# Moving some stick-breaking products from the vector engine to GpSimd in a Hymba encoder block

## The chip, the cores and the metric

The kernel runs on one core of a Trainium2 chip. A core has a matrix engine (PE, with its weight loads shown apart as PEld), a vector engine (DVE), a scalar engine for activations (ACT), GpSimd (POOL) and a queue engine (SP) that here issues nearly all DMAs. Each engine carries out its own instructions strictly in the order in which they stand in its program; semaphores hold an instruction until what it needs is done. The metric is the device time of one execution in microseconds (us), smaller is better. The kernel before takes 2757.65 us (median of 3 runs, 2754.74 to 2759.51).

## The reference

One layer of an encoder block over 2048 tokens of width 1024, batch 1: an RMS norm, one projection into six parts, differential attention (4 heads), stick-breaking attention (8 heads of width 64), an output projection added to the input, then a second norm and a gated feed-forward of width 2816, added again. The part that the change touches is stick-breaking attention, for query t and key s before it:

```python
z = jnp.einsum('bqhd,bkhd->bhqk', qb, k).astype(jnp.float32) * scale
mask = (k_pos[None, :] < q_pos[:, None])[None, None]
log_1mb = jnp.where(mask, jax.nn.log_sigmoid(-z), 0.0)
rem = lax.cumsum(log_1mb, axis=3, reverse=True) - log_1mb
a = jnp.where(mask, jnp.exp(jax.nn.log_sigmoid(z) + rem), 0.0)
return jnp.einsum('bhqk,bkhd->bqhd', a.astype(v.dtype), v)
```

In words: the weight of key s is sigmoid(z) at s, times the product of sigmoid(-z) over all keys between s and t.

## The kernel before

Work runs in groups g = 0 to 7. Groups 0 to 3 are one differential head each, groups 4 to 7 two stick-breaking heads each. While the attention of group g runs, the projection of group g + 1 is interleaved with it; beside g = 7, which has no projection after it, stands the output projection (`out_proj`, L766 its matmuls) with the second norm and the operands of the feed-forward (`post`, `x_ops`). The feed-forward follows, bound by PE throughout. Nearly every f32 operand is kept as a pair of f16 values, hi and lo, and each product of pairs is three matmuls.

One step of stick-breaking attention (`stage_a`) takes a block of 128 queries, one of two heads and up to 1024 keys: a tile. There are 48 tiles and 80 chunks of up to 512 keys in a group. A chunk goes through:

- PE computes the scores into a PSUM bank `sc` (L453; on the diagonal one more matmul, L455). There are four such banks.
- ACT writes sigmoid(-z) to the SBUF tile `om` (L559) and then sigmoid(z) over the scores in PSUM (L560).
- DVE runs the product from the last key back to the first in place in `om` (L562, a scan; its second operand `sc` is read and not used).
- DVE multiplies sigmoid(z) from PSUM with the scan shifted by one key, into the SBUF tile `be` (L563).

When the tile's chunks are done (`split_t`), ACT or POOL casts `be` to f16 (L89 on ACT), POOL subtracts to get the lo half (L98), and SP issues a DMA transpose of the pair into `aT` (L408). PE multiplies `aT` with the values (L463, `stage_b`), five tiles later in the written order. The SBUF tiles `be` and `om` come from one ring of nine (`z4`), the f16 pairs from a ring of three (`s16`), `aT` from a ring of five.

Two things set the order. The program is written as generators that interleave the attention with the projection; a scheduler then simulates it and fixes the order on each engine. And which engine gets a piece of work is often picked at build time by a planner: a load in ns for ACT (A), DVE (D) and POOL (P), set to zero at every fourth query block (`level`), added to by `note` for work with a fixed place and by `pick` for the rest, which takes the engine with the least load after it:

```python
def pick(**cost):
    e = min(cost, key=lambda k: load[k] + cost[k] * KW[k])
    load[e] += cost[e] * KW[e]
    return e
```

The planner also places the projection's PSUM evictions. `split_psum` picks ACT (L332) or DVE (L334) for the f16 hi half, and DVE always does the lo half (L335). `tt`, whose instructions all stand at L98, picks DVE or POOL for the sums of `x_ops`.

Of the kernel before, what the change touches and what calls it, by code (L numbers as in the profile page):

```python
# [15 lines left out]
AF = mybir.ActivationFunctionType  # L16
ALU = mybir.AluOpType
# [4 lines left out]
S, D, P = 2048, 1024, 128  # L22
# [37 lines left out]
def block(tc, a, out):  # L60
    nc = tc.nc
    PE, ACT, DVE, POOL, SP = nc.tensor, nc.scalar, nc.vector, nc.gpsimd, nc.sync
    top = ExitStack()
    with top:
# [8 lines left out]
        def note(e, ns):  # L73
            load[e] += ns * KW[e]
# [6 lines that stand above are left out]
        def level():  # L81
            for k in load:
                load[k] = 0.0
# [16 lines left out]
        def pri(k):  # L100
            def deco(f):
                @functools.wraps(f)
                def g(*args):
                    with tc.high_priority(PRI[k]) if PRI[k] else nullcontext():
                        return f(*args)
                return g
            return deco

        def nm(s):
            uid[0] += 1  # L110
            return f"{s}{uid[0]}"
# [144 lines left out]
        with ExitStack() as ph1:  # L256
# [6 lines left out]
            def z4():  # L263
                return zp.tile([P, 1028], F32, tag="z4", bufs=ZB, name=nm("z4"))
# [137 lines left out]
            @pri("spl")  # L402
            def split_t(src, n, he="ADP", le="DP"):
                s16 = s16p.tile([P, 2048], F16, tag="s16", bufs=SB, name=nm("s16"))
                to16(s16[:, :n], src, n, he)
                tt(s16[:, n : 2 * n], src, s16[:, :n], ALU.subtract, n, le)
                aT = sp.tile([P, 16, P], F16, tag="aT", bufs=AB, name=nm("aT"))
                SP.dma_start_transpose(aT[:, : 2 * n // P, :], s16[:, : 2 * n])  # L408
                return aT
# [36 lines left out]
            def fq(g, i):  # L446
                k = 2 if g == NG - 1 else 4
                return (i % k, k)

            @pri("sc")  # L450
            def score_chunk(G, sc, i, q, m, w, cut=False):
                for o in range(2):
                    PE.matmul(sc[:, : 128 * w].rearrange("p (t n) -> p t n", n=P), lhsT=G["q"][i // 4][:, 2 - 2 * o + m, i % 4, :], rhs=G["k"][q][:, m, 0:w, :], start=o == 0, stop=o == 1)  # L453
                if cut:
                    PE.matmul(sc[:, 128 * w - P : 128 * w], lhsT=idb[:], rhs=tri[:], start=False, stop=True, skip_group_check=True)  # L455

            @pri("pv")
            def pv(G, yp, y0, aT, b, n, o, wd, start, stop):
                nb = n // P
                for j in range(nb):  # L460
                    v = G["v"][2 * b + j // 4][:, j % 4, :]
                    for q, (a_, v_) in enumerate(((j, o), (j, o + wd), (nb + j, o))):
                        PE.matmul(yp[:, y0 : y0 + wd], lhsT=aT[:, a_, :], rhs=v[:, v_ : v_ + wd], start=start and j == 0 and q == 0, stop=stop and j == nb - 1 and q == 2, skip_group_check=True)  # L463
# [77 lines left out]
            def sb_attn(g, G):  # L541
                last = {}

                @pri("at")
                def stage_a(i, m, b):
                    L = (i + 1) * 128
                    n = min(1024, L - 1024 * b)
                    be, om = z4(), z4()
                    if b == i // 8:
                        DVE.memset(om[:, n : n + 1], 8192.0)  # L550
                    else:
                        DVE.tensor_copy(om[:, n : n + 1], last[m][:, 0:1])
                    last[m] = om
                    for c in range((n - 1) // 512, -1, -1):
                        lo, hi = 512 * c, min(512 * c + 512, n)
                        w = hi - lo
                        sc = ps.tile([P, 512], F32, tag="sc", bufs=4, name=nm("sc"))
                        score_chunk(G, sc, i, 2 * b + c, m, w // P, b == i // 8 and hi == n)
                        ACT.activation(om[:, lo:hi], sc[:, :w], AF.Sigmoid, scale=G["nkz"][:])  # L559
                        ACT.activation(sc[:, :w], sc[:, :w], AF.Sigmoid, scale=G["kz"][:])  # L560
                        ov = om[:, lo:hi][:, ::-1]
                        DVE.tensor_tensor_scan(ov, ov, sc[:, :w], om[:, hi : hi + 1], op0=ALU.mult, op1=ALU.bypass)  # L562
                        DVE.tensor_tensor(be[:, lo:hi], sc[:, :w], om[:, lo + 1 : hi + 1], ALU.mult)  # L563
                        note("A", 1.7 * w + 400)
                        note("D", 3.15 * w + 350)
                    return n, split_t(be[:, :n], n, "A", "P")

                ypd = {}

                def stage_b(i, m, b, n, aT):  # L570
                    r, k = fq(g, i)
                    if i // k not in ypd:
                        ypd[i // k] = ps.tile([P, 512], F32, tag="yp", name=nm("yp"))
                    yp = ypd[i // k]
                    pv(G, yp, P * r + 64 * m, aT, b, n, 128 * m, 64, r == 0 and m == 0 and b == i // 8, r == k - 1 and m == 1 and b == 0)
                    if m == 1 and b == 0 and r == k - 1:
                        finish(g, G, i, k, yp)
                        G["fin"] = i + 1

                pend = []  # L580
                done = 0
                for i in range(NT):
                    if i % 4 == 0:
                        level()
                    for b in range(i // 8, -1, -1):
                        for m in range(2):
                            n, aT = stage_a(i, m, b)
                            pend.append((i, m, b, n, aT))
                            if len(pend) > PD:
                                stage_b(*pend.pop(0))  # L590
                            done += n // P + CS
                            yield done / (272 + 48 * CS), (i + 1 if b == 0 and m == 1 else i)
                for u in pend:
                    stage_b(*u)
# [640 lines left out]
```

## Time and profile before

| what | value |
|---|---|
| median of the timed runs | 2757.65 us |
| the profiled execution's own time | 2755.86 us |
| its span, first to last instruction | 2754.1 us |
| busy over the span: PE, DVE, POOL, ACT | 90%, 73%, 53%, 49% |
| mean granted PE clock | 0.966 |
| first to last scan (L562), that is groups 4 to 7 | 612.6 to 1395.6 us |

A row of groups reads: line, engine, operation, output and input tiles, shape and count, then busy us and the mean ns of one, then the us that the engine stood idle just before them and what ended it. A row of waits reads: who waited, for whom, us in total, times, longest. A row of stretches gives, for a stretch of time, its length, the busy us of PE, PEld, DVE, ACT and POOL with the number of instructions in brackets, the granted clock, the share of the DMA engines that packets took (several may overlap, so it can exceed 1), and GB/s.

### The profile page before, as it was taken

Reading aid. Unit: us, or ns where it says so; the run is one execution under the profiler, and the core shown is the slowest. Engines: PE = TensorE matmul, PEld = TensorE weight load, DVE = VectorE, ACT = ScalarE, POOL = GpSimd, SP = SyncE. Lnnn points to the kernel's source line nnn. Section 1 sums busy time; section 2 is a strip of 40 time slices with the busy share of each in tenths; the row PEclk is TensorE's granted clock in tenths of the full one; section 3 lists DMA queues with packets and bytes.
Section 4 is the critical chain, followed back from the end, with each engine's and each line's share of the span. In section 5 each row is a group of like instructions: output and inputs, shape, how many; then the busy total and the mean of one; then the engine's idle time right before and its main releaser. Section 6 shows DMA issues by size and latency. Waiting matters only on the chain. (4 is left out here: it accounts for less than half of the span.)

```text
span 2754.1 us, 45485 instructions
## 1 busy us (share of the span) xinstructions
PE 2491.4 (90%) x17084; PEld 1411.9 (51%) x17084; DVE 1997.4 (73%) x3782; ACT 1361.3 (49%) x2543; POOL 1447.6 (53%) x1008
## 2 busy tenths in 40 slices
PE   7998989888888786888989899999999999999998
PEld 4665555555555453457775444444444444444443
DVE  6898879787889989986655877777785544444445
ACT  4665656566878778765644535444352212111121
POOL 2578767655455545546565656565574232322323
PEclk9999999999999987999999999999999999999999
DMA  6788787789999988987797675656658834635534
GB/s 225 201 170 184 148 189 163 173 172 203 196 217 191 198 175 156 199 196 208 199 272 273 218 241 199 220 196 226 235 182 307 315 146 164 229 136 198 207 121 167
DMA packets 649133, 551.91 MB, mean 200 GB/s; under 512 B 506624, under 2 KB 574208, under 8 KB 638672
## 3 DMA queue, kind: packets, MB, share of 16 engines
q1 hardware_dynamic: 647088, 546.92, 72.0%
q8 instruction: 134, 2.20, 0.3%
q0 software_dynamic: 512, 1.36, 0.2%
q10 hardware_dynamic: 1312, 0.72, 0.1%
q14 instruction: 87, 0.71, 0.1%
HBM read 265.27 MB, written 151.52 MB: 151 GB/s over the span
## 5 line engine op out<-in xcount | busy, mean ns | idle before, releaser
L98 POOL TENSOR_TENSOR s<-z,s 128x1024 f16<-128x1024 f32 (+7 forms) x288 | 473.9, 1653 | 334.1 <-ACT s L89 291.2
L325 PE MATMUL pj<-w,xt 128*128 128x384 f16 x3072 | 572.2, 334 | 29.3 <-DVE st L335 12.1
L325 PEld LDWEIGHTS <-xt 128*128 128x128 f16 x3072 | 300.2, 100 | 239.9 <-issue 37.3
L453 PE MATMUL sc<-kT,qT 128*128 128x512 f16 (+3 forms) x1280 | 348.7, 363 | 72.0 <-DVE z L563 33.0
L1041 PE MATMUL pd<-wd,act 128*128 128x512 f16 x1848 | 406.0, 379 | 3.4 <-DVE hs L1047 2.4
L562 DVE TENSOR_TENSOR_SCAN z<-z,sc 128x512 f32<-128x512 f32 (+3 forms) x320 | 355.5, 1113 | 69.4 <-ACT sc L560 67.5
L463 PE MATMUL yp<-v,aT 128*128 128x64 f16 (+1 forms) x4896 | 282.0, 208 | 76.4 <-DMA aT<-s 75.7
L463 PEld LDWEIGHTS <-aT 128*128 128x128 f16 x4896 | 246.5, 102 | 165.1 <-DMA aT<-s 101.7
L943 PEld LDWEIGHTS <-wg 128*128 128x128 f16 x1848 | 182.3, 99 | 247.3 <-issue 37.3
L1041 PEld LDWEIGHTS <-act 128*128 128x128 f16 x1848 | 180.7, 98 | 222.3 <-issue 4.6
L943 PEld LDWEIGHTS <-wu 128*128 128x128 f16 x1848 | 181.8, 98 | 219.7 <-issue 7.2
L98 POOL TENSOR_TENSOR hs<-hs,cu 128x512 f32<-128x512 f32 x132 | 166.8, 1268 | 239.8 <-DVE cu L1047 86.3
L98 POOL TENSOR_TENSOR act<-cg,act 128x512 f16<-128x512 f32 x117 | 166.6, 1437 | 231.4 <-ACT act L999 125.1
L98 POOL TENSOR_TENSOR fst<-fst 128x512 f32<-128x512 f32 x97 | 182.5, 1882 | 157.3 <-DVE wd L220 85.9
L1047 DVE SCALAR_TENSOR_TENSOR hs<-pd,c,hs 128x512 f32<-128x512 f32 x192 | 142.3, 749 | 163.0 <-PE pd L1041 161.5
L89 ACT CAST s<-z 128x384 f16<-128x384 f32 (+7 forms) x216 | 170.2, 789 | 151.5 <-DMA aT<-s 61.9
L559 ACT ACTIVATE z<-sc,c 128x512 f32<-128x512 f32 (+3 forms) x320 | 203.3, 635 | 10.2 <-PE sc L453 6.7
L563 DVE TENSOR_TENSOR z<-sc,z 128x512 f32<-128x512 f32 (+3 forms) x320 | 193.4, 606 | 8.1
L560 ACT ACTIVATE sc<-sc,c 128x512 f32<-128x512 f32 (+3 forms) x320 | 195.6, 611 | 0.0
L999 ACT CAST act<-cg 128x512 f16<-128x512 f32 x132 | 81.3, 616 | 222.1 <-DVE cg L1005 175.8
L766 PE MATMUL po<-wo,mt 128*128 128x256 f16 x1536 | 182.0, 277 | 6.9 <-DVE xf L769 4.9
L943 PE MATMUL pm<-X,wg 128*128 128x512 f16 x792 | 179.1, 379 | 0.2 <-ACT bx L1116 0.2
(233 smaller groups left out, 4026.5 us busy)
## 6 DMA issues: line engine op xcount, KB each, us to landing
xt<-xs SPq DMA_DIRECT2D x112, 512.0 KB, 4.4
hs<-hd SPq DMA_DIRECT2D x96, 512.0 KB, 4.3
hd<-hs SPq DMA_DIRECT2D x80, 512.0 KB, 3.5
split<-wg SPq DMA_DIRECT2D x11, 1792.0 KB, 11.4
split<-wu SPq DMA_DIRECT2D x11, 1792.0 KB, 10.3
split<-wd SPq DMA_DIRECT2D x11, 1792.0 KB, 10.5
wg<-split SPq DMA_DIRECT2D x11, 1792.0 KB, 7.2
wd<-split SPq DMA_DIRECT2D x11, 1792.0 KB, 8.2
```

Of the source, the lines that this page charges most:

```text
L89: ACT.copy(dst, src)
L98: (DVE if e == "D" else POOL).tensor_tensor(dst, a_, b_, op)
L325: PE.matmul(pj[:, :384], lhsT=xv[:, xi, kt, :], rhs=G["w"][:, wi, kt, :], start=n == 0, stop=n == 23)
L453: PE.matmul(sc[:, : 128 * w].rearrange("p (t n) -> p t n", n=P), lhsT=G["q"][i // 4][:, 2 - 2 * o + m, i % 4, :], rhs=G["k"][q][:, m, 0:w, ...
L463: PE.matmul(yp[:, y0 : y0 + wd], lhsT=aT[:, a_, :], rhs=v[:, v_ : v_ + wd], start=start and j == 0 and q == 0, stop=stop and j == nb - 1 a ...
L559: ACT.activation(om[:, lo:hi], sc[:, :w], AF.Sigmoid, scale=G["nkz"][:])
L560: ACT.activation(sc[:, :w], sc[:, :w], AF.Sigmoid, scale=G["kz"][:])
L562: DVE.tensor_tensor_scan(ov, ov, sc[:, :w], om[:, hi : hi + 1], op0=ALU.mult, op1=ALU.bypass)
L563: DVE.tensor_tensor(be[:, lo:hi], sc[:, :w], om[:, lo + 1 : hi + 1], ALU.mult)
L766: PE.matmul(po[:, sl], lhsT=mt[:, kt, P * xi : P * xi + P], rhs=wos[2 * h + n][wi][:, kt, :], start=q == 0, stop=q == 23)
L943: PE.matmul(ps_[:].rearrange("p (t n) -> p t n", n=P), lhsT=wv[:, wo, wi, 128 * kt : 128 * kt + 128], rhs=X[xo][:, :, xi, kt, :], start=st ...
L1041: PE.matmul(po[:], lhsT=act[:, ao, xi, 128 * j : 128 * j + 128], rhs=W["d"][:, wo, wi, :], start=start and u == 0 and q == 0, stop=u == nu ...
```

## The change

For each chunk the planner now picks who multiplies. If it is DVE, nothing changes. If it is POOL, the second sigmoid is written to `be` in SBUF and POOL multiplies it in place. The fixed load of DVE per chunk is lowered by what was its product. From L560 on, lines of the changed kernel are two higher: the second sigmoid is L562, the scan L564, the product L565.

```diff
                         ACT.activation(om[:, lo:hi], sc[:, :w], AF.Sigmoid, scale=G["nkz"][:])
-                        ACT.activation(sc[:, :w], sc[:, :w], AF.Sigmoid, scale=G["kz"][:])
+                        e = pick(D=1.04 * w + 155, P=2.4 * w + 100)
+                        beta = sc[:, :w] if e == "D" else be[:, lo:hi]
+                        ACT.activation(beta, sc[:, :w], AF.Sigmoid, scale=G["kz"][:])
                         ov = om[:, lo:hi][:, ::-1]
                         DVE.tensor_tensor_scan(ov, ov, sc[:, :w], om[:, hi : hi + 1], op0=ALU.mult, op1=ALU.bypass)
-                        DVE.tensor_tensor(be[:, lo:hi], sc[:, :w], om[:, lo + 1 : hi + 1], ALU.mult)
+                        (DVE if e == "D" else POOL).tensor_tensor(be[:, lo:hi], beta, om[:, lo + 1 : hi + 1], ALU.mult)
                         note("A", 1.7 * w + 400)
-                        note("D", 3.15 * w + 350)
+                        note("D", 2.08 * w + 200)
```

Since the planner's loads change, other picks change with them: 64 evictions of the projection go from ACT (L332) to DVE (L334), 19 of 256 columns and 45 of 128; and beside g = 7 the sums of `x_ops` go from POOL to DVE, 6 of 1024 columns and 12 of 512. Three places show how the order moves.

POOL, near the end of group 5. Tiles named z4 are `be` and `om`, s16 is the f16 pair; the number after the underscore tells tiles apart. Before, POOL holds only the subtractions:

```order
L98 TENSOR_TENSOR s162130_12206<-z42126_12188,s162130_12206 128x768
L98 TENSOR_TENSOR s162137_12244<-z42133_12227,s162137_12244 128x1024
L98 TENSOR_TENSOR s162147_12318<-z42143_12301,s162147_12318 128x1024
L98 TENSOR_TENSOR s162153_12365<-z42149_12347,s162153_12365 128x896
L98 TENSOR_TENSOR s162159_12412<-z42155_12394,s162159_12412 128x896
```

and now:

```order
L565 TENSOR_TENSOR z42126_12188<-z42126_12188,z42127_12189 128x512
L565 TENSOR_TENSOR z42133_12227<-z42133_12227,z42134_12228 128x512 x2
L98 TENSOR_TENSOR s162130_12206<-z42126_12188,s162130_12206 128x768
L565 TENSOR_TENSOR z42143_12301<-z42143_12301,z42144_12302 128x512
L98 TENSOR_TENSOR s162137_12244<-z42133_12227,s162137_12244 128x1024
L565 TENSOR_TENSOR z42155_12394<-z42155_12394,z42156_12395 128x512
L98 TENSOR_TENSOR s162147_12318<-z42143_12301,s162147_12318 128x1024
L98 TENSOR_TENSOR s162153_12365<-z42149_12347,s162153_12365 128x896
```

The products of the next tile or two now stand between a tile's cast on ACT and its subtraction on POOL.

DVE, shortly before that place, with pj the projection's PSUM tile, v and st its f16 outputs. The scan is written SCALAR_TENSOR_TENSOR in the program. Before:

```order
L562 SCALAR_TENSOR_TENSOR z42103_12015<-z42103_12015,sc2104_12017 128x512
L563 TENSOR_TENSOR z42102_12014<-sc2104_12017,z42103_12015 128x512
L552 COPY z42109_12049<-z42095_11949 128x1
L562 SCALAR_TENSOR_TENSOR z42103_12015<-z42103_12015,sc2105_12024 128x512
L563 TENSOR_TENSOR z42102_12014<-sc2105_12024,z42103_12015 128x512
L562 SCALAR_TENSOR_TENSOR z42109_12049<-z42109_12049,sc2110_12051 128x512
L563 TENSOR_TENSOR z42108_12048<-sc2110_12051,z42109_12049 128x512
```

and now:

```order
L564 SCALAR_TENSOR_TENSOR z42103_12015<-z42103_12015,sc2104_12017 128x512
L335 SCALAR_TENSOR_TENSOR st2250_13090<-pj2285_13242,st2250_13090 128x4x64
L220 SCALAR_TENSOR_TENSOR w162254_13125<-wst2253_13121,sW2258_13129,w162254_13125 128x1536
L564 SCALAR_TENSOR_TENSOR z42109_12049<-z42109_12049,sc2110_12051 128x512
L564 SCALAR_TENSOR_TENSOR z42103_12015<-z42103_12015,sc2105_12024 128x512
L334 TENSOR_SCALAR v2251_13091<-pj2309_13391 128x2x64
L565 TENSOR_TENSOR z42108_12048<-sc2110_12051,z42109_12049 128x512
```

The two products of tile 12014 are gone from DVE, those of tile 12048 stay, and an eviction (L334) that ACT did is there instead.

POOL, beside group 7, in the sums of one pair of row blocks (x16 is their f16 output). Before:

```order
L93 TENSOR_SCALAR x162944_17902<-z42912_17656 128x2x512
L151 TENSOR_TENSOR xrs2940_17885<-xrs2940_17885,mh1_77 128x1
L98 TENSOR_TENSOR s162932_17755<-z42928_17737,s162932_17755 128x768
L98 TENSOR_TENSOR x162944_17902<-z42912_17656,x162944_17902 128x2x512
L98 TENSOR_TENSOR z42943_17901<-z42913_17657 128x512
L98 TENSOR_TENSOR z42913_17657<-z42913_17657,z42912_17656 128x512
L98 TENSOR_TENSOR z42943_17901<-z42913_17657 128x512
L98 TENSOR_TENSOR z42912_17656<-z42943_17901,z42912_17656 128x512
L98 TENSOR_TENSOR x162945_17910<-z42913_17657,x162945_17910 128x2x512
```

and now:

```order
L565 TENSOR_TENSOR z42928_17737<-z42928_17737,z42929_17738 128x512
L98 TENSOR_TENSOR s162932_17755<-z42928_17737,s162932_17755 128x768
L98 TENSOR_TENSOR z42943_17901<-z42913_17657 128x512
L98 TENSOR_TENSOR z42913_17657<-z42913_17657,z42912_17656 128x512
L565 TENSOR_TENSOR z42948_17922<-z42948_17922,z42949_17923 128x512
L98 TENSOR_TENSOR x162946_17914<-z42943_17901,x162946_17914 128x2x512
```

Two of the four narrow sums and the two wide subtractions into 17902 and 17910 are on DVE now, the cast (L93) on ACT, and products stand between what is left.

## The prediction

> **What bounds the kernel now.** I read the page's span and busy line first, then the busy time by stretches, then PE's waits inside the stretch that the change touches.
>
> ```profile
> span 2754.1 us, 45485 instructions
> PE 2491.4 (90%) x17084; PEld 1411.9 (51%) x17084; DVE 1997.4 (73%) x3782; ACT 1361.3 (49%) x2543; POOL 1447.6 (53%) x1008
> ```
>
> The profiled execution took 2755.86 us, 1.76 us of it outside its span; the median of the three timed runs is 1.79 us above it. Averaged over the span PE is the bound. The change is in the stick-breaking groups, and their stretch looks different. The first row is ordinary differential attention, the next three hold the stick-breaking groups g = 4, 5 and 6 (80 scans each), then g = 7 together with the output projection, then g = 4 to 6 as one. Columns: stretch, length, busy us of each engine with its count, granted PE clock, DMA share, GB/s.
>
> ```profile
> 100.00:600.00 500.00, 453.66 (x3569) 289.89 (x3566) 426.76 (x1273) 300.74 (x787) 348.15 (x250) 0.98 0.80 173
> 612.00:797.00 185.00, 155.64 (x1545) 98.35 (x1543) 160.45 (x298) 142.82 (x277) 98.95 (x62) 0.98 1.02 205
> 797.00:965.00 168.00, 135.19 (x1411) 84.68 (x1409) 151.42 (x265) 133.99 (x254) 84.69 (x55) 0.93 0.96 194
> 965.00:1120.00 155.00, 119.14 (x1228) 73.28 (x1226) 143.20 (x245) 128.31 (x242) 82.75 (x54) 0.83 0.88 169
> 1120.00:1400.00 280.00, 239.23 (x2457) 184.42 (x2454) 209.29 (x362) 176.05 (x322) 153.30 (x107) 0.95 0.82 199
> 612.00:1120.00 508.00, 409.98 (x4176) 256.31 (x4174) 455.07 (x807) 405.12 (x770) 266.38 (x169) 0.92 0.96 191
> ```
>
> From 612 to 1120 us DVE is busy 455.07 of 508 us (0.896) and PE only 410 (0.807), where it reached 453.66 of 500 (0.907) before. PE's own waits there:
>
> ```profile
> PE yp L463 <- DMA aT<-s: 36.4, 33, 3.5
> PE sc L453 <- DVE z L563: 25.4, 29, 1.4
> PE sc L453 <- DVE z L550: 11.0, 14, 1.7
> PE sc L453 <- DVE z L552: 8.7, 9, 1.8
> PE pj L325 <- DMA xt<-xs: 8.0, 6, 3.2
> PE pj L325 <- DVE st L335: 5.8, 7, 1.7
> ```
>
> DVE ends 50.9 us of them (25.4 + 11.0 + 8.7 + 5.8): the next scores wait for a PSUM bank that DVE still reads. The transposed probabilities (aT) end 36.4 us. So in this stretch **DVE bounds, with the transposes close behind**.
>
> **The change part by part.** Counted from the two built programs, 148 of the 320 products (L563) go to POOL, 46% and not a third: 35 in each of g = 4, 5, 6 (28 of 512 columns, 1 of 384, 4 of 256, 2 of 128) and 43 in g = 7 (33, 3, 4, 3). The prices, from g = 4 to 6:
>
> ```profile
> L563 DVE TENSOR_TENSOR z<-sc,z 128x512 f32<-128x512 f32 x163 | 111.9, 687 | 4.6
> L563 DVE TENSOR_TENSOR z<-sc,z 128x384 f32<-128x384 f32 x24 | 13.3, 552 | 0.7
> L563 DVE TENSOR_TENSOR z<-sc,z 128x256 f32<-128x256 f32 x24 | 10.0, 418 | 0.4
> L335 DVE SCALAR_TENSOR_TENSOR st<-pj,st 128x256 f16<-128x256 f32 x46 | 18.5, 403 | 2.1 <-ACT st L332 2.0
> L335 DVE SCALAR_TENSOR_TENSOR v<-pj,v 128x128 f16<-128x128 f32 x47 | 12.9, 276 | 5.8 <-ACT v L332 5.8
> L332 ACT ACTIVATE st<-pj 128x256 f16<-128x256 f32 x47 | 18.7, 398 | 12.2 <-DVE v L335 12.1
> L332 ACT ACTIVATE v<-pj 128x128 f16<-128x128 f32 x47 | 13.9, 298 | 4.0 <-PE pj L325 3.3 <-PE yp L463 0.5
> ```
>
> *Off DVE:* 84 x 0.687 + 3 x 0.552 + 12 x 0.418 + 6 x 0.29 (estimate, the next step down) = 66 us. *Back onto DVE:* the planner's new loads send 19 + 45 evictions (L332) from ACT to DVE. DVE has no such row here; a DVE pass over the same PSUM tile takes 0.403 and 0.276, so 19 x 0.403 + 45 x 0.276 = 20 us (bounds: nothing where they fall into DVE's 53 idle us, 25 at a quarter more each). **Net, DVE loses 46 us of 455.** ACT loses 19 x 0.398 + 45 x 0.298 = 21 us; its second sigmoid in a POOL chunk writes SBUF, which the first sigmoid does at 0.700 against 0.677:
>
> ```profile
> L559 ACT ACTIVATE z<-sc,c 128x512 f32<-128x512 f32 x166 | 116.2, 700 | 5.0 <-PE sc L453 3.5 <-PE sc L455 1.4
> L560 ACT ACTIVATE sc<-sc,c 128x512 f32<-128x512 f32 x165 | 111.8, 677 | 0.0
> L98 POOL TENSOR_TENSOR z<-z,z 128x512 f32<-128x512 f32 x7 | 9.0, 1282 | 5.0 <-DVE z L98 4.6
> L98 POOL TENSOR_TENSOR fst<-fst 128x512 f32<-128x512 f32 x97 | 182.5, 1882 | 157.3 <-DVE wd L220 85.9
> ```
>
> That is 2 us over 84 chunks, hidden by the 21. *Onto POOL:* nothing in this stage has the product's exact place; the same form (two f32 operands in SBUF, 512 columns) takes 1.282 us in g = 7's stretch and, on the page, 1.882 as fst in the feed-forward. I take 1.282, from the same neighbours (the scan there too reads its second operand from PSUM), and for the narrow ones 0.96, 0.64 and 0.32 (estimates, in proportion to their width): 84 x 1.282 + 3 x 0.96 + 12 x 0.64 + 6 x 0.32 = 120 us. POOL then holds 266 + 120 = 386 us.
>
> What can each resource do with this over the 508 us?
> - DVE at its present 0.896: 409/0.896 = 457, a gain of 51.
> - PE at its 0.907 of the earlier stage: 410/0.907 = 452, a gain of 56.
> - The DMA engines: 0.96 x 508 = 488 us of packets, not reduced. The highest share held for long is 1.02 over the 185 us from 612: 488/1.02 = 478, a gain of 30.
> - POOL: its highest share over any 100 us, 0.777 from 400 to 500, gives 386/0.777 = 497, a gain of 11:
>
> ```profile
> 400.00:500.00 100.00, 91.06 (x774) 59.73 (x773) 92.22 (x266) 64.90 (x168) 77.72 (x50) 0.98 0.78 164
> POOL s L98 <- ACT s L89: 214.0, 103, 5.7
> ACT s L89 <- DMA aT<-s: 35.3, 30, 4.4
> ```
>
> POOL's share is no ceiling, though: 214 of its 242 idle us were waits for ACT's cast (L89), and the new products stand in just those gaps. So the ends are 11 and 51, and I take the DMA bound between them, **30 us**. The changed order supports it: a tile's values (L463) follow its scores by 10.2 score chunks on average in these groups, not 7.9, which at 508/240 = 2.1 us a chunk is 4.9 us more cover. A product on POOL adds 1.282 - 0.687 = 0.6 us and, at worst, the 2.2 us subtraction queued ahead of it. Queued behind it on POOL is the next tile's subtraction, and behind that its transpose on SP's queue.
>
> One wait stays. In 144 of the 148 chunks the scan still waits for the second sigmoid, so DVE's 30.5 us before L562 in this stage remain. The PSUM bank is free after the scan and not the product, 0.69 us earlier, which is where PE's 50.9 us shrink.
>
> ```profile
> DVE z L562 <- ACT sc L560: 30.5, 39, 2.1
> ```
>
> *g = 7, 1120 to 1400 us:* products leave DVE for 33 x 0.687 + 3 x 0.552 + 4 x 0.418 + 3 x 0.29 = 27 us and put 49 on POOL; in exchange the planner moves output-side sums (post, L98) to DVE, 6 of 1024 columns at 1.328 and about 12 of 512 at 0.67 (estimate: half), 16 us, which with 4 casts takes 33 off POOL:
>
> ```profile
> L98 DVE TENSOR_TENSOR x<-z,x 128x1024 f16<-128x1024 f32 x4 | 5.3, 1328 | 0.0
> L98 POOL TENSOR_TENSOR x<-z,x 128x1024 f16<-128x1024 f32 x8 | 17.0, 2130 | 0.1
> ```
>
> DVE -11, POOL +16. DVE is busy 0.75 here and PE 0.854, so the value is 0, between 11 gained and 16 lost. After about 1480 us both programs have the same instructions in the same order on every engine: what is gained before comes out whole at the end. Sum: 2755.86 - 30 = 2725.9 for a profiled execution, 2757.65 - 30 = **2728 us** as a median.
>
> **The rivals.**
>
> *The nine buffers take DVE's place (slower).* Each tile takes two of nine z4 buffers, the last freed by POOL's subtraction, so 4.5 tiles are in flight. At 508/144 = 3.53 us a tile, a pair may be held 15.9 us. The bare chain is two sigmoids (1.38), two scans (2 x 1.273), a product (1.282), a cast (1.051) and a subtraction (2.183): 8.4 us, 7.4 left for queueing.
>
> ```profile
> L562 DVE TENSOR_TENSOR_SCAN z<-z,sc 128x512 f32<-128x512 f32 x164 | 208.7, 1273 | 19.4 <-ACT sc L560 18.5 <-PE sc L455 0.4
> L89 ACT CAST s<-z 128x1024 f16<-128x1024 f32 x57 | 59.9, 1051 | 34.3 <-issue 10.1 <-DVE z L563 9.3 <-DMA aT<-s 8.0
> L98 POOL TENSOR_TENSOR s<-z,s 128x1024 f16<-128x1024 f32 x60 | 130.9, 2183 | 118.0 <-ACT s L89 113.8 <-DMA aT<-s 3.0 <-DVE c L170 1.1
> ```
>
> Two subtractions ahead on POOL (4.4) and a sigmoid pair and a cast ahead on ACT (2.4) would use 6.8 of it. Past 15.9 us each further us costs 144/4.5 = 32 us; at 16.5, +20: 2778 us. For it: the in-order hops ACT, POOL, ACT, POOL. Against: the products stand in POOL's gaps, and the sum of these queues still fits. Chance 0.21.
>
> *The transposes hold the pace anyway.* PE waits 36.4 us for aT already and ACT's casts 35.3 for the s16 buffers that the transposes free. If the DMA share stays at 0.96, the relief of DVE turns into these waits: 2755 us, within the 0.2% (5.5 us) that a measurement here can tell from no change. Against: 1.02 was held for 185 us. Chance 0.13.
>
> *POOL and DVE slow each other.* fst at 1.882 shares its stage with DVE passes that read two SBUF operands (L220). At that price the products cost 176 us and POOL holds 442; kept by its in-order waits at 0.85, above any share seen here, it needs 442/0.85 = 520, +12: 2770 us. Against: scan and product on DVE both take one operand from PSUM, and z<-z,z beside them stayed at 1.282. Chance 0.06. The Trainium skill (SBUF — State Buffer, Who interferes with whom) has this as an exclusive lock: DVE with two SBUF inputs blocks a GpSimd reader for a whole instruction, with one it does not. By that rule only the moved sums of g = 7 and the weight splits can collide; the two prices of 1.282 and 1.882 agree with it.
>
> **How the numbers follow.** The forecast has 0.60, and its own range is 2707 (51 gained) to 2747 (11). The rivals have 0.21, 0.13 and 0.06. The low end adds g = 7's 11 us to the 51: 2696; the high end stops just short of the buffer rival's price, 2776. Faster by over 0.2%: 0.60; within: 0.13 and a little of the rest, 0.14; slower: 0.26.
>
> **What would show it.** Right: from the first scan of g = 4 to the last of g = 6 about 478 us, DVE near 0.86 busy, POOL near 0.8, L565 on POOL at 1.28, PE's waits for DVE's products under 30 us and for aT no larger than now, DMA share near 1.02. Wrong: ACT's L559 waiting for POOL (buffers), L565 near 1.9 (port), aT waits above 60 us (transposes), or the stretch of g = 7 longer than 296 us.

## The result, and the profile after

The changed kernel takes 2738.77 us (median of 4 runs, 2737.14 to 2744.19) against 2756.45 of the kernel before in the same comparison: a ratio of 0.9939, 95% interval 0.9924 to 0.9954. That is 17.7 us faster, where 30 were forecast. The profiled execution took 2740.35 us, 15.5 less than that of before. Medians here and below leave out one execution each of two kernels that was far slower than its others (10911.55 and 2947.71 us).

Span and busy time of the page after:

```profile
span 2738.6 us, 45565 instructions
PE 2479.7 (91%) x17084; PEld 1409.0 (51%) x17084; DVE 1952.9 (71%) x3716; ACT 1347.7 (49%) x2483; POOL 1570.8 (57%) x1134
```

DVE lost 44.5 us and POOL gained 123.2 over the span. Where the time went is read by stretches, cut in each kernel at its own scans: the first scan of g = 4, the last ones of g = 4, 5 and 6 (the 80th, 160th and 240th scan), the last of g = 7. The kernel before, with g = 4, 5, 6, the three together, then g = 7 (columns as in the prediction's table of stretches):

```profile
612.60:800.60 188.00, 156.81 (x1557) 99.13 (x1555) 163.31 (x303) 144.94 (x281) 100.19 (x63) 0.97 1.02 206
800.60:969.80 169.20, 136.67 (x1435) 86.15 (x1436) 152.59 (x270) 134.99 (x254) 85.82 (x55) 0.92 0.96 191
969.80:1129.70 159.90, 122.39 (x1238) 74.39 (x1236) 148.27 (x251) 130.54 (x244) 83.30 (x55) 0.84 0.88 170
612.60:1129.70 517.10, 415.87 (x4226) 259.67 (x4225) 464.17 (x820) 410.46 (x779) 269.31 (x171) 0.91 0.95 190
1129.70:1395.80 266.10, 228.54 (x2339) 176.77 (x2338) 196.06 (x345) 167.99 (x310) 147.03 (x103) 0.95 0.83 202
```

The changed kernel, cut in the same way:

```profile
611.80:791.60 179.80, 155.68 (x1547) 99.07 (x1545) 149.64 (x293) 137.42 (x256) 132.54 (x96) 0.97 1.04 207
791.60:958.10 166.50, 135.45 (x1409) 85.23 (x1407) 137.64 (x254) 129.10 (x236) 119.46 (x90) 0.93 1.00 199
958.10:1112.30 154.20, 118.92 (x1284) 74.85 (x1281) 132.36 (x229) 128.40 (x235) 118.96 (x90) 0.87 0.92 177
611.80:1112.30 500.50, 410.06 (x4234) 259.15 (x4231) 419.64 (x772) 394.92 (x725) 370.96 (x274) 0.93 0.99 195
1112.30:1379.80 267.50, 225.84 (x2353) 176.74 (x2354) 192.00 (x323) 169.12 (x305) 175.00 (x129) 0.96 0.83 202
```

The gain sits in g = 4 to 6: 517.1 to 500.5, 16.6 us, of which 8.2, 2.7 and 5.7 in the three groups. g = 7 is 1.4 longer, and from its last scan to the end it is 1358.3 us before and 1358.8 after. With 0.8 less ahead of g = 4 this makes up the 15.5 us.

Of the 44.5 us that DVE no longer works in g = 4 to 6, only 16.6 came out: it is idle for 80.9 us (500.5 - 419.64) and not 52.9 (517.1 - 464.17). The waits of that stretch, changed kernel:

```profile
ACT s L89 <- DMA aT<-s: 66.1, 44, 3.5
ACT z L559 <- POOL z L565: 1.3, 1, 1.3
PE yp L463 <- DMA aT<-s: 48.9, 43, 3.7
DVE z L564 <- ACT sc L562: 32.4, 29, 5.1
DVE z L564 <- ACT z L562: 26.4, 19, 3.8
PE pj L325 <- DVE st L335: 8.2, 6, 2.1
PE sc L453 <- DVE z L564: 13.6, 16, 1.6
PE sc L453 <- DVE z L550: 7.2, 10, 1.9
PE sc L453 <- DVE z L552: 3.9, 7, 0.8
PE sc L453 <- DVE z L565: 3.3, 5, 1.0
```

Read from the bottom. PE's scores wait less for DVE now: 28.0 us in the last four rows, where L563, L550 and L552 had 45.1 in the prediction's rows. DVE's scans wait for ACT's second sigmoid 58.8 us (32.4 + 26.4) and not 30.5. That is 28.3 more, as much as all the idle time that DVE gained (28.0). ACT's cast waits for an f16 buffer that a transpose has not freed yet 66.1 us and not 35.3, and PE for transposed probabilities 48.9 and not 36.4. The time that DVE got back turned into waits that lead to ACT and to the transposes; what each of them costs, the rows do not tell.

The new and moved instructions of the same stretch, by shape:

```profile
L565 POOL TENSOR_TENSOR z<-z,z 128x512 f32<-128x512 f32 x83 | 91.5, 1105 | 55.0 <-DVE z L564 49.8 <-DVE z L552 1.8 <-DVE z L550 1.2
L334 DVE TENSOR_SCALAR v<-pj 128x128 f16<-128x128 f32 x38 | 10.5, 277 | 4.7 <-PE pj L325 3.3 <-PE yp L463 1.2
L334 DVE TENSOR_SCALAR st<-pj 128x256 f16<-128x256 f32 x18 | 7.5, 415 | 0.0
```

The product on POOL takes 1.105 us on average, less than the 1.282 taken from its nearest relative. The evictions that came back to DVE cost 0.277 and 0.415 us each, 18.0 us together for the 56 that fall into this stretch.

### The profile page after: what moved, and what is told of

It reads as the page before. It is cut to its first block, busy times and chain, and to the rows that moved or that the text cites. A ratio compares the mean times of both kernels' runs of the same rounds, so it can differ in the third digit from the quotient of the medians.

```text
span 2738.6 us, 45565 instructions
## 1 busy us (share of the span) xinstructions
PE 2479.7 (91%) x17084; PEld 1409.0 (51%) x17084; DVE 1952.9 (71%) x3716; ACT 1347.7 (49%) x2483; POOL 1570.8 (57%) x1134
## 5 line engine op out<-in xcount | busy, mean ns | idle before, releaser
L98 POOL TENSOR_TENSOR s<-z,s 128x1024 f16<-128x1024 f32 (+7 forms) x288 | 477.4, 1667 | 105.2 <-ACT s L89 100.0
L564 DVE TENSOR_TENSOR_SCAN z<-z,sc 128x512 f32<-128x512 f32 (+3 forms) x320 | 353.3, 1113 | 84.4 <-ACT sc L562 43.0
L453 PE MATMUL sc<-kT,qT 128*128 128x512 f16 (+3 forms) x1280 | 341.5, 359 | 48.7 <-DVE z L564 14.9
L98 POOL TENSOR_TENSOR hs<-hs,cu 128x512 f32<-128x512 f32 x132 | 166.8, 1268 | 241.8 <-DVE cu L1049 86.6
L98 POOL TENSOR_TENSOR act<-cg,act 128x512 f16<-128x512 f32 x117 | 166.5, 1435 | 236.1 <-ACT act L1001 129.8
L98 POOL TENSOR_TENSOR fst<-fst 128x512 f32<-128x512 f32 x97 | 182.8, 1884 | 152.5 <-DVE wd L220 85.0
L559 ACT ACTIVATE z<-sc,c 128x512 f32<-128x512 f32 (+3 forms) x320 | 206.5, 648 | 27.2 <-PE sc L453 21.4
L565 POOL TENSOR_TENSOR z<-z,z 128x512 f32<-128x512 f32 (+3 forms) x148 | 152.4, 1032 | 98.8 <-DVE z L564 83.4
L945 PE MATMUL pm<-X,wu 128*128 128x512 f16 x792 | 179.1, 379 | 0.0
## 6 DMA issues: line engine op xcount, KB each, us to landing
split<-wu SPq DMA_DIRECT2D x11, 1792.0 KB, 10.4
```

The lines of the kernel that those rows point to most:

```text
L98: (DVE if e == "D" else POOL).tensor_tensor(dst, a_, b_, op)
L565: (DVE if e == "D" else POOL).tensor_tensor(be[:, lo:hi], beta, om[:, lo + 1 : hi + 1], ALU.mult)
L945: PE.matmul(ps_[:].rearrange("p (t n) -> p t n", n=P), lhsT=wv[:, wo, wi, 128 * kt : 128 * kt + 128], rhs=X[xo][:, :, xi, kt, :], start=st ...
```

## The experiments

Two theories stood against each other after this profile. **Transposes:** relieved of its products, DVE runs into the service of the transposes; the growing waits of ACT and PE for them are the lost gain. **Something of the change's own:** the ring of f16 buffers, the evictions given back to DVE, POOL late with its subtractions, too little lag between scores and values, or DVE's wait for the second sigmoid holds the stretch. The lengths of stretches below are of g = 4 to 6, cut as above. Each ratio here is against runs of the kernel before on the same chip, whose median was 2758.28 to 2760.38 us; so kernels of different comparisons are set against each other by their ratios.

### Half the transposed columns, after and before

The part of the edit that matters:

```diff
-                SP.dma_start_transpose(aT[:, : 2 * n // P, :], s16[:, : 2 * n])
+                h = n // P
+                SP.dma_start_transpose(aT[:, : (h if one else 2 * h), :], s16[:, (n if one else 0) : 2 * n])
```

Here `one` is set for stick-breaking attention alone, and the values' matmuls read the lo half in place of both: the hi half is left out of the result, and the matmuls are as many as before. The first text is of the changed kernel, the second of the kernel before.

> The changed kernel with half the transposed columns in stick-breaking attention: only the lo half of each tile is transposed, after POOL's subtraction as before, and stands in for the hi half in the products with the values (the hi half is left out of the output). The chain of hand-offs is unchanged, the DMA work of the transposes is halved. Theory transfer rate: the stretch of groups 4 to 6, 500 us in the changed kernel, falls to 475 or less, PE's wait for aT there from 49 to under 30 us, ACT's for s16 from 66 to under 30. Theory hand-offs (each tile goes DVE, POOL, ACT, POOL, SP in order, and the queues set the pace): 488 to 500 us, the waits only move.

> The kernel before with the same halved transposes. It was 517 us in that stretch with DVE 0.90 busy. If DVE sets its pace: 508 to 517 us. If the transposes held it too, it falls as far as the changed kernel's, 25 us or more, and the change's gain stays near 17 us with them halved.

The changed kernel then takes 2714.27 us (0.984, 0.982 to 0.9859), the kernel before 2740.01 (0.9931, 0.9909 to 0.9953). Stretches of the changed kernel with half the columns, g = 4, 5 and 6:

```profile
614.80:788.40 173.60, 148.66 (x1504) 95.63 (x1503) 151.52 (x294) 136.52 (x256) 131.11 (x96) 0.99 0.83 172
788.40:949.10 160.70, 137.33 (x1470) 86.73 (x1469) 138.55 (x252) 129.60 (x235) 120.33 (x89) 0.96 0.71 148
949.10:1101.50 152.40, 114.34 (x1246) 70.39 (x1244) 133.47 (x226) 127.96 (x234) 117.22 (x89) 0.88 0.61 127
```

and of the kernel before with half the columns:

```profile
615.60:803.00 187.40, 159.09 (x1583) 102.28 (x1581) 165.21 (x303) 142.95 (x280) 100.34 (x63) 0.96 0.79 169
803.00:970.00 167.00, 134.02 (x1410) 83.64 (x1407) 152.39 (x268) 133.82 (x256) 85.36 (x55) 0.95 0.65 134
970.00:1129.30 159.30, 120.54 (x1250) 73.47 (x1251) 148.73 (x250) 130.94 (x246) 83.23 (x55) 0.85 0.54 114
```

Without the change, halving the transposes is worth 3.4 us here (517.1 to 513.7). With it, 13.8 (500.5 to 486.7). Put the other way, the change gains 16.6 us with whole transposes and 27.0 with halved ones: 5.6 more in g = 4, 3.6 in g = 5, 1.2 in g = 6. So DVE does bound first, and the transposes take some 10 us of what its relief would give. The medians point the same way, g = 7 included: the change is worth 25.7 us with halved transposes (2740.01 - 2714.27) and 17.7 with whole ones. The spread of the runs leaves this difference of 8.0 uncertain by some 6 us (an estimate). The granted clock differs too with half the columns, by +0.01 to +0.03 in the groups of the changed kernel and by -0.01 to +0.03 in those of the kernel before, and no run separates its part. Of what the kernel before gains in the median (2760.22 to 2740.01), most is in g = 7, which takes 252.3 us and not 266.1. A transpose takes 4.5 us from issue to landing in the changed kernel's stretch, and 3.1 with half the columns (medians).

The waits of the changed kernel with half the columns (its lines are one higher: the scan is L565, the second sigmoid L563, the values L464):

```profile
ACT s L89 <- DMA aT<-s: 41.3, 28, 4.1
PE yp L464 <- DMA aT<-s: 30.7, 30, 3.2
DVE z L565 <- ACT sc L563: 24.1, 24, 2.5
DVE z L565 <- ACT z L563: 10.1, 16, 1.6
```

All three waits shrink together: ACT for transposes 66.1 to 41.3, PE for them 48.9 to 30.7, and DVE for ACT 58.8 to 34.2. So the waits did not only move, as the hand-offs theory had it, but the stretch did not come down to the 475 us or less of the other theory either: 486.7 lies between them. DVE's busy share is 0.870 (423.5 of 486.7) with a DMA share of 0.61 to 0.83: with half of the transposes gone the rest still waits for each other.

### A fourth f16 buffer, after and before

```diff
-QB, KB, ZB, AB, SB, PD = 4, 7, 9, 5, 3, 5
+QB, KB, ZB, AB, SB, PD = 4, 7, 9, 5, 4, 5
-                y = sp.tile([P, 512], F32, tag="y", bufs=2, name=nm("y"))
+                y = sp.tile([P, 512], F32, tag="y", bufs=1, name=nm("y"))
```

One `y` buffer less makes room for it. The first text is of the changed kernel, the second of the kernel before.

> The changed kernel with four s16 buffers instead of three (the room comes from one y buffer instead of two, used once per eight tiles). Theory ring: in the changed kernel ACT's casts wait 66 us for an s16 buffer in groups 4 to 6 (35 before), because POOL's products stand between a tile's cast and its subtraction and so hold the pair longer; a fourth buffer takes most of this away: 2715 to 2728 us, ACT's wait for aT under 25 us. Theory transfer rate: the transposes themselves set the pace, a fourth buffer only moves the wait to PE: 2734 to 2744 us, PE's wait for aT over 60 us.

> The kernel before with the same four s16 buffers. Both theories have DVE as its bound, so little moves: 2748 to 2758 us. If it gains as much as the changed kernel does from the fourth buffer (10 us or more), the ring was a limit before the change as well and not something that the change brought.

Changed kernel 2753.2 us (0.9974, 0.9961 to 0.9987), kernel before 2754.33 (0.9976, 0.9966 to 0.9987). Stretch and waits of the changed kernel with four buffers:

```profile
615.80:1115.70 499.90, 412.98 (x4265) 262.84 (x4266) 423.43 (x776) 396.12 (x726) 366.43 (x273) 0.93 0.98 198
PE yp L463 <- DMA aT<-s: 49.4, 44, 3.0
ACT s L89 <- DMA aT<-s: 25.8, 18, 4.2
DVE z L564 <- ACT sc L562: 22.4, 25, 2.6
DVE z L564 <- ACT z L562: 12.9, 15, 4.0
```

ACT's wait falls by 40 us and DVE's by 23.5, as with half the columns, and the stretch does not move (499.9 against 500.5): PE's wait for aT stays at 49.4. So ACT's wait for a buffer does not hold the stretch, and these 23.5 us of DVE's wait for ACT do not either: DVE's idle time fell by only 4.4 us (80.9 to 76.5), as other waits took its place. That the whole is slower than the changed kernel comes from elsewhere: in g = 7 (273.3 against 267.5) and behind it (1366.7 against 1358.8); the last run below, the same program up to g = 7 as the changed kernel's, has the 4 us more ahead of g = 4 (615.8 against 611.8) too. The kernel before with four buffers has 620.8 ahead and 1366.4 behind. The missing `y` buffer, which both share, may be why; but the run with more lag, further down, has both `y` buffers and 1365.0 behind, so this stays open.

### The same products without the evictions, and the evictions without the products

The edit of the changed kernel, without the table and its counter:

```diff
-                        e = pick(D=1.04 * w + 155, P=2.4 * w + 100)
+                        e = WHO[0 if g < 7 else 1][who[0]]
+                        who[0] += 1
-                        note("D", 2.08 * w + 200)
+                        note("D", 3.15 * w + 350)
```

`WHO` lists the 148 chunks of the changed kernel, and the planner's load of DVE is that of before, so evictions and sums stay where they were.

> The same 148 products on POOL, from a table, with the planner's loads noted as in the kernel before, so that the evictions stay on ACT and the sums beside group 7 on POOL. Theory give-back: the 20 us of evictions that came back to DVE ate the missing gain: 2722 to 2730 us. Theories ring and transfer rate: DVE no longer sets the pace and ACT, which the casts hold up, gets 21 us more: 2736 to 2748 us; beside group 7 POOL holds 49 us more instead of 16, which may add up to 10.

2744.93 us, 0.9941 (0.9929 to 0.9954); the stretch is 503.7. Then the evictions alone: in the kernel before, the planner picks as in the changed one, and the product is made on DVE whatever it picked.

Added and replaced lines against the kernel before:

```diff
+                        e = pick(D=1.04 * w + 155, P=2.4 * w + 100)
+                        beta = sc[:, :w]
-                        note("D", 3.15 * w + 350)
+                        note("D", 2.08 * w + 200)
```

> The planner's picks of the changed kernel, but all 320 products stay on DVE as before: only the 64 evictions and the sums beside group 7 move to DVE. It prices the give-back where DVE bounds: 20 us in groups 4 to 6 at DVE's share of 0.9 are 15 to 22 us, and up to 16 more beside group 7: 2770 to 2790 us. If it is under 2762, evictions cost DVE's path nothing and the sum should not have counted them.

2755.08 us, 0.9981 (0.9972 to 0.999): not slower, but a little faster. The stretch, and DVE's wait for the second sigmoid in it:

```profile
614.00:1130.50 516.50, 414.77 (x4254) 260.83 (x4253) 478.13 (x873) 396.15 (x723) 266.19 (x170) 0.92 0.95 190
DVE z L564 <- ACT sc L562: 15.1, 25, 2.1
```

DVE works 14.0 us more (478.13, a share of 0.926) in the same time (516.5 against 517.1): its wait for ACT, which is rid of these evictions, is 15.1 and not 30.5. So the moved evictions cost nothing, and DVE's 0.896 was no ceiling.

### POOL relieved, after and before

```diff
-                tt(s16[:, n : 2 * n], src, s16[:, :n], ALU.subtract, n, le)
+                if le == "P":
+                    note("P", 2.45 * n + 80)
+                    POOL.tensor_scalar(s16[:, n : 2 * n], src, 0.0, 0.0, op0=ALU.mult, op1=ALU.add)
+                else:
+                    tt(s16[:, n : 2 * n], src, s16[:, :n], ALU.subtract, n, le)
```

POOL's subtraction becomes a cheaper pass of one operand that writes zeros: the lo half of these f16 pairs is left out.

> The changed kernel with POOL relieved and nothing else moved: in stick-breaking attention the lo half is written as zeros by a one-operand pass instead of the subtraction (the low halves are left out of the output). That pass takes about 1.1 us per 1024 columns where the subtraction takes 2.2, so POOL holds some 110 us less in groups 4 to 6. Theory POOL (its in-order queue makes the tiles late): the stretch falls from 500 to under 485 us and PE's wait for aT under 35. Theory transfer rate: 493 to 502 us, PE's wait for aT stays above 42.

> The kernel before, with the subtraction on GpSimd in its casts replaced by a pass that reads one operand and writes zeros (the low half of the stick-breaking probabilities is left out). Theory 'GpSimd's subtractions already paced g = 7 before the change': g = 7 goes from 266.1 to 247 to 255, and the time to 2738 to 2747. Theory 'the change itself made GpSimd the pace of g = 7': g = 7 stays at 260 to 268 and the time within 5 us of the kernel before. In both g = 4 to 6 stays at 510 to 518, since GpSimd is not its pace.

Changed kernel 2720.72 us (0.9858, 0.9835 to 0.9881), kernel before 2763.9 (1.0017, 1.0007 to 1.0028). The changed kernel's stretches with this, g = 4 to 6 and g = 7:

```profile
615.80:1118.10 502.30, 416.06 (x4257) 260.98 (x4254) 416.29 (x770) 394.86 (x724) 263.95 (x275) 0.92 0.98 196
1118.10:1366.90 248.80, 221.75 (x2300) 173.22 (x2301) 189.82 (x325) 169.53 (x307) 135.56 (x129) 0.96 0.93 216
```

POOL works 107 us less in g = 4 to 6 and nothing is gained there (502.3): neither POOL's time nor its place ahead of the transposes holds that stretch. In g = 7 it is worth 18.7 us after the change (267.5 to 248.8) and nothing before it (266.1 to 272.7).

### Products on DVE in g = 7

```diff
-                        e = pick(D=1.04 * w + 155, P=2.4 * w + 100)
+                        e = pick(D=1.04 * w + 155, P=(2.4 if g < NG - 1 else 99.0) * w + 100)
```

> The changed kernel, but in g = 7 every product stays on DVE; in g = 4 to 6 the products go to GpSimd as before this edit. With GpSimd relieved of its subtractions g = 7 took 248.8 us and not 267.5. Theory 'GpSimd paces g = 7 and the 43 products there (some 45 us of it) cost': g = 7 comes down to 247 to 256 and the time to 2720 to 2729. Theory 'the products in g = 7 are worth nothing, as the prediction had it': g = 7 stays at 262 to 270 and the time at 2734 to 2742. Theory 'DVE bounds in g = 7': its stretch passes 275 and the time 2745. The stretch of g = 4 to 6 should stay at 498 to 503 by all three.

2738.03 us, 0.9928 (0.9913 to 0.9943). g = 7 takes 265.9 us against 267.5, and g = 4 to 6, where the order is the same, 500.7 against 500.5. The planner here puts the sums of `x_ops` back on POOL as well. The 43 products in g = 7 are worth nothing that can be measured.

### More lag, another order on ACT, and the order alone

Values seven tiles behind their scores and not five (`PD` 5 to 7):

> The changed kernel with a tile's values written seven tiles behind its scores instead of five, all rings as they are. Theory hand-offs: more cover for a longer chain, PE's wait for aT under 35 us and the stretch 485 to 495 us. Theory transfer rate: the ring of five aT tiles fills and nothing is gained, 498 to 510 us.

2751.95 us, 0.9978 (0.9965 to 0.999). The stretch stays at 501.5 and ACT's wait for transposes is 72.0; PE's wait for aT falls only from 48.9 to 42.5. More lag does not shorten the stretch. Of the 10.9 us by which the profiled execution is longer, 6.2 lie behind g = 7 (1365.0 us and not 1358.8).

The second sigmoid of a POOL chunk behind its scan:

```diff
-                        ACT.activation(beta, sc[:, :w], AF.Sigmoid, scale=G["kz"][:])
                         ov = om[:, lo:hi][:, ::-1]
+                        if e == "D":
+                            ACT.activation(beta, sc[:, :w], AF.Sigmoid, scale=G["kz"][:])
                         DVE.tensor_tensor_scan(ov, ov, sc[:, :w], om[:, hi : hi + 1], op0=ALU.mult, op1=ALU.bypass)
+                        if e == "P":
+                            ACT.activation(beta, sc[:, :w], AF.Sigmoid, scale=G["kz"][:])
```

> The changed kernel, but in the chunks whose product is on GpSimd the second sigmoid is written behind the scan, so that the scan waits for the first sigmoid alone. The same 148 products are on GpSimd, and 65 evictions on DVE instead of 64. After the change DVE's scans waited 32.4 + 26.4 us for ACT in g = 4 to 6. Theory 'the waits of DVE for ACT hold the stretch': they fall under 30 us, the stretch of g = 4 to 6 goes from 500.5 to 485 to 492, and the time to 2725 to 2732. Theory 'the transposes hold it': these waits fall too, but the stretch stays at 497 to 503, PE's wait for aT and ACT's for s16 stay at or above 48.9 and 66.1, and the time is 2735 to 2742.

2763.09 us, 1.0013 (1.0005 to 1.0022): the whole gain is gone. Stretch and waits (the scan is L565, the second sigmoid of a POOL chunk L567, of a DVE chunk L564):

```profile
616.00:1126.50 510.50, 412.45 (x4234) 258.07 (x4232) 423.35 (x772) 398.15 (x723) 371.82 (x274) 0.92 0.95 192
DVE z L565 <- ACT sc L564: 46.9, 35, 3.8
DVE z L565 <- ACT z L559: 12.3, 14, 1.9
ACT z L567 <- DVE z L565: 17.3, 25, 1.8
ACT z L567 <- DVE z L550: 14.6, 12, 3.8
ACT z L567 <- DVE z L552: 6.8, 8, 2.4
PE sc L453 <- ACT z L567: 15.2, 17, 2.8
```

Neither theory had this. DVE's waits for ACT did not shrink (46.9 + 12.3 = 59.2 against 58.8), because ACT now stands 38.7 us in its own queue waiting for DVE, and the sigmoids of the next chunks stand behind that. The late sigmoid also keeps its PSUM bank, which the scan no longer frees, and PE's scores wait 15.2 us for it, where they wait for no second sigmoid in the changed kernel. So the run does not tell what DVE's wait is worth by itself; it shows that this order has no such slack: with these two new waits the stretch is 10 us longer, and which of them costs it was not separated. (The profiled execution took 2755.36, the shortest of this kernel's.)

Last, the order alone: one load of the output projection's weights in g = 7 is written one tile earlier. Up to the last scan of g = 6, every engine has the same instructions in the same order in both programs.

```diff
-WT = (4, 7, 10)
+WT = (4, 7, 9)
```

> The changed kernel with one number of the schedule moved: the last of the three loads of the output projection's weights in g = 7 is written one tile earlier (tile 9 and not 10). The work is the same; the order in g = 7 differs on every engine, and up to there nothing does. Theory 'the 249 to 273 us that g = 7 took in the builds so far have real causes': g = 7 stays at 263 to 271 and the time at 2735 to 2742. Theory 'order alone moves g = 7 by as much': g = 7 leaves 260 to 274 on either side. In both g = 4 to 6 stays at 499 to 502.

2740.4 us, 0.9934 (0.9921 to 0.9947). g = 7 takes 265.9, so this edit does not move it. The other number is the useful one, the stretch of g = 4 to 6:

```profile
615.40:1112.10 496.70, 404.46 (x4234) 256.25 (x4231) 420.50 (x772) 394.29 (x725) 369.47 (x274) 0.95 1.00 197
```

The same work in the same order takes 496.7 at a granted clock of 0.95 and 500.5 at 0.93. The first scan stands 3.6 us later here (615.4 against 611.8), and both reach the last scan of g = 6 at the same time (1112.1 and 1112.3). So a difference under 4 us between two such profiles tells nothing. By that measure the listed chunks' 503.7, the four buffers' 499.9, the relieved POOL's 502.3 and the lag's 501.5 are all the changed kernel's stretch, and the 3.4 us of halved transposes in the kernel before are not told from nothing either. The main result does not hang on where the first scan stands: counted from the span's start, the last scan of g = 6 comes 17.4 us earlier with the change (1129.7 to 1112.3) and 27.8 earlier with halved transposes (1129.3 to 1101.5), again 10.4 apart.

No kernel that computes all of the reference beat the changed one by more than its interval.

## Why the prediction was right, and where not

**What bounds (DVE, with the transposes close behind): right.** Halved transposes alone give 3.4 us, the change alone 16.6, both 30.4 (517.1 to 486.7). Only with DVE relieved are the transposes worth much in this stretch.

**Off DVE and back onto it: right in size, wrong in what the return costs.** Net 44.5 us against 46 forecast, 18.0 for the 56 evictions in the stretch against 20 for all 64. But the 20 was subtracted from the gain; moved by themselves, the evictions cost no time, and left out, they bring none (0.9941 against 0.9939).

**POOL's product: too dear.** 1.105 us and not 1.282. The price was that of another form: the sums z<-z,z of the kernel before take 1.26 to 1.30 us each, the one with nothing on DVE beside it 1.26. POOL gained 101.7 us of work in the stretch (269.31 to 370.96) against 120 forecast. Its share is 0.741 there. As the prediction held, POOL's share was no ceiling: with 107 us less the stretch stays.

**The sum, step "488/1.02 = 478, a gain of 30": this is the one that failed.** It took a DMA share as a ceiling, pooled over three groups that stand at different shares. By group, the rule would have given nothing in g = 4, which stood at 1.02 already, 10 in g = 5 (169.2 x 0.96/1.02 = 159.2) and 22 in g = 6 (159.9 x 0.88/1.02 = 138.0). Measured were 8.2, 2.7 and 5.7, at shares of 1.04, 1.00 and 0.92. A bound that is wrong in each group gave a gain of the right order only in sum, and that is luck. What the runs show in its place: the waits for transposes grew when DVE stopped holding the tiles back (ACT's from 35.3 to 66.1, PE's from 36.4 to 48.9), while the share rose to no more than 1.00 and 0.92 in g = 5 and 6, and with half the transposes the change gains 27.0 and not 16.6 us. That is 10.4 of the missing 13.4 us. Through which wait the transposes hold the stretch is not shown; it is not ACT's for a buffer alone, which a fourth buffer took away for nothing. The other 3.0 are within the 4 us that the same program differs by. One part was plain arithmetic: the forecast of "about 478" for the time between scans took off 30 from 508 us, the round cut, where the scans are 517.1 apart; it should have read 487.

**"DVE's 30.5 us before L562 remain": wrong by a factor of two.** They became 58.8. The wait was named, but taken as fixed; it is what the relieved engine runs into next. It is no price, though: a fourth buffer took 23.5 us of it away and shortened nothing.

**PE's waits and the shares.** For DVE under 30 us: right for the scores, 28.0. The 50.9 us that were to shrink also counted 5.8 for L335, a wait of the projection and not of the scores; with its 8.2 now they are 36.2. For aT no larger: wrong, 48.9 and not 36.4, short of the 60 that would have spoken for the transposes alone. The longer distance between scores and values in the written order, taken as 4.9 us more cover, did not keep this wait down, and more lag does not shorten the stretch either. DVE stood at 0.838 (419.64 of 500.5) where 0.86 was forecast, and the DMA share at 0.99 and not 1.02.

**g = 7 at 0, nothing behind it: right.** +1.4 and +0.5 us; with its products back on DVE it is 1.6 shorter.

**The rivals.** The nine buffers took nobody's place: ACT's L559 waited for POOL 1.3 us in all. The transposes did not hold the pace alone, but they took 10.4 us, a third of the forecast's gain. DVE slowed POOL's product once among the 105 of g = 4 to 6 and seven times among the 43 of g = 7, some 6 us in all (see the end), and the mean in g = 4 to 6 stays at 1.105.

**What stays open.** g = 7 took 249 to 273 us in these kernels. With POOL relieved it fell to 248.8 after the change and not before it, and with its products off POOL it did not fall, as if DVE and POOL had to be relieved both; but the kernel before with a fourth f16 buffer (253.3) and with halved transposes (252.3) got there too, and no run tells what these have in common. Nor is it shown what holds g = 4 to 6 at 486.7 with halved transposes, where DVE works 42.8 us less than before the change (466.3 to 423.5) and only 27.0 come out; DVE's and ACT's waits for each other are the largest left on DVE, and the one run that aimed at them made new ones.

## What to carry to other kernels

A share of busy time that was once held is not a ceiling: split the stretch into its stages first, and if the rule gives one stage no gain and another too much, it is not the rule. When an engine is relieved, follow the chain of waits one step on and test what it costs: here DVE's new idle time (28.0 us) was as long as its added wait for ACT (28.3), but a fourth buffer that took 23.5 us of this wait away gave nothing, and halving the transposes gave 13.8. An instruction moved later on an in-order engine takes everything behind it along, and holds what it reads: freeing DVE's scan of a sigmoid made ACT wait 38.7 us and PE 15.2, and cost the whole gain.

## What the runs showed of the hardware

A product of two f32 operands in SBUF, 128x512, in place on the first of them, takes POOL 1.08 to 1.10 us when DVE does not get in its way; other sums of that size took 1.282 and 1.882 on average. Eight of the 148 products take longer, one in g = 6 and seven in g = 7. From the timeline of the changed kernel (start, us, instruction), five on POOL and, in the second list, three on DVE:

```profile
1102.45 2.08 POOL L565 TENSOR_TENSOR z<-z,z 128x512 f32<-128x512 f32 x1
...
1123.14 0.86 POOL L565 TENSOR_TENSOR z<-z,z 128x384 f32<-128x384 f32 x1 [1.10 <-DVE z L564]
...
1158.06 1.84 POOL L565 TENSOR_TENSOR z<-z,z 128x384 f32<-128x384 f32 x1
1161.47 1.08 POOL L565 TENSOR_TENSOR z<-z,z 128x512 f32<-128x512 f32 x1
...
1313.06 1.46 POOL L565 TENSOR_TENSOR z<-z,z 128x512 f32<-128x512 f32 x1 [1.41 <-DVE z L564]
```

```profile
1101.61 1.96 DVE L220 SCALAR_TENSOR_TENSOR wo<-z,sW,wo 128x1024 f16<-128x1024 f32 x1
1156.72 2.46 DVE L220 SCALAR_TENSOR_TENSOR wo<-z,sW,wo 128x1024 f16<-128x1024 f32 x1
1312.90 0.67 DVE L98 TENSOR_TENSOR z<-z 128x512 f32<-128x512 f32 x1
```

The three slow products, at 1102.45, 1158.06 and 1313.06, start while DVE runs a weight split (L220) or one of the sums of `x_ops` (L98), which read two operands from SBUF; the other two, with neither beside them, take 0.86 and 1.08. It is so for all 148: four start during an L220 and four during an L98 on DVE, and these are the eight slow ones. The other 140, of which 58 start during a scan, are not slow. The Trainium skill (SBUF — State Buffer, Who interferes with whom) says that a DVE instruction with two SBUF inputs contends with a GpSimd instruction that reads SBUF, and that one with at most one, outside its two-port modes, does not. These rows agree: the 384 columns that start 1.12 us before the split's end take 1.84 and not 0.86, about 1 us more. And they show how long POOL is held: each of the seven slow products of 512 columns ends 0.95 to 0.96 us after the DVE instruction that it met (the one at 1102.45 at 1104.53, its split at 1103.57), whether it started 0.5 or 1.1 us before that end. So it is not slowed throughout; it waits for DVE's end. It stays small here, some 6 us of POOL's time, because few products meet such an instruction.
